# A decoder layer in split float32r: the second norm's broadcast as two float32r products for half the tokens, and two first transfers in the other order

## The chip, the cores and the metric

One core of one Trainium2 chip. The metric is the device time of one execution in microseconds, as the median of several runs. The profile is of one execution, with a span from the first to the last instruction that is a little shorter than its device time.

## The reference, cut to what matters

One layer (DEPTH = 1) of a decoder on x of 1024 tokens by 1024 features, all float32:

```python
u = rms_norm(h, attn_norm[i])
mix = swa_mixer(u, swa_w_qkv[j], swa_sinks[j], swa_w_o[j])
h = h + mix
h = h + squared_relu_mlp(rms_norm(h, mlp_norm[i]), mlp_w_up[i], mlp_w_down[i])
...
return rms_norm(h, final_norm)
```

`rms_norm` is `x * rsqrt(mean(x*x) + 1e-6) * g`. `swa_mixer` is attention in a window of 128 tokens, 16 query heads of 64 on 2 key and value heads, with a sink and a distance penalty for each head. `squared_relu_mlp` is `relu(h @ w_up)**2 @ w_down` with 4096 hidden features.

## The kernel before

Features lie on the partitions and tokens along the row, in tiles of 128 x 1024 (eight of them for x). Products are float32r in three parts: a value is split into a high part (a cast by ACT) and the rest (a subtraction by DVE), and `mm3` (line 131) adds high x high, high x low and low x high. The stages follow each other:

- **Keys and values** (lines 169 to 240): for each of the eight tiles k of x, ACT scales by the first norm's weights into `xh`, DVE makes the rest `xl`, and PE adds the products with tile k of the key and value weights into `psk` and `psv`. ACT also squares x, DVE adds the squares up in `ssq`, and small products with ones turn them into the sum for each token. The norm itself is applied later to keys, values and scores.
- **Attention** with the query products put between its steps, then **the output product** `o` (two blocks of 512 tokens, called hf = 0 and hf = 1, each for eight blocks m of features), which DVE adds onto `h`.
- **Second norm, and the up and down products** of the MLP in Strassen's form (seven products of half blocks, X, Y, Z in the profile being their banks), then the last norm.

The first transfers. Line 170 issues `gn` (all three norms' weights, 128 x 24) on ACT's queue and line 171 the first 256 columns of the key weights, `wk_r`, behind it. All other loads here are issued by SP: `xr`, the tiles of x (line 214; the first two tiles in halves of 512 tokens), and the other pieces of the key and value weights (`kvload`, line 188). `wsplit` (line 119) is the cast `wk_h` on ACT and the rest `wk_l` on DVE. The program writes the split of the first key weights ahead of the first `xh`; in this part the order on an engine is chosen by a scheduler, later (where `ordered` is set) it is the program's.

The second norm for hf = 0 runs under the output products of hf = 1. In the loop over m at line 917, with m = 0, `stat_part` puts small products with ones (`n2s`) between the twelve products of `oblock(0, 1)`; `stat_sum` (line 660) makes the reciprocal root `rn2` of each token with `rstd` (line 146: a root on ACT, then a Newton step on DVE, `n_st` in the profile) and a diagonal tile `dg` = identity x `rn2` with `diag` (line 157, DVE). With m = 1, behind the twelve products of `oblock(1, 1)`, `stat_bcast` (line 668) multiplies `dg` by ones (`bcast`, line 161: one float32 product of 128 x 512), so that every partition has the value of each token (`n2b`). DVE then makes `x` = h * gn * n2b, of which ACT and DVE make `xb_h` and `xb_l`. For hf = 1 the same happens later, under the first up products.

The first norm does its own broadcast (line 493) with a high part `rnh` and a rest `rnl` of the reciprocal root, two diagonals `dg1` in float32r, and two products with `ones_r`, a float32r copy of ones.

Of the kernel before, what the change touches and what calls it, by code (L numbers as in the profile page):

```python
# [6 lines left out]
F32 = mybir.dt.float32  # L7
F32R = mybir.dt.float32r
I32 = mybir.dt.int32
AF = mybir.ActivationFunctionType  # L10
ALU = mybir.AluOpType
# [3 lines left out]
P = 128  # L15
# [47 lines left out]
def trunk(tc, xT, gains, wqkv, wo, wup, wdn, bias_d, sinks_d, ident_d, mask_d, grow_d, outT, outB):  # L63
# [10 lines left out]
    nc = tc.nc  # L74
    v, s, g, pe = (Ordered(tc, e) for e in (nc.vector, nc.scalar, nc.gpsimd, nc.tensor))
# [14 lines left out]
    def wtile(dt, name):  # L90
        return big.tile([P, 1024], dt, tag="W", name=name, bufs=6)

    def rtile(name):
        return big.tile([P, 1024], F32, tag="R", name=name, bufs=3)
# [16 lines left out]
    def mm(out, lhsT, rhs, start, stop, **kw):  # L111
        pe.matmul(out, lhsT=lhsT, rhs=rhs, start=start, stop=stop, **kw)
        if tiny:
            tiny.pop(0)()
# [31 lines left out]
    def rstd(ps, n, name):  # L146
        st = const.tile([P, 4, NB], F32, tag="st", name=f"{name}_st", bufs=3)
        var, y0, b_, y = (st[:, i, 0:n] for i in range(4))
        s.activation(y, ps[:, 0:n], AF.Sqrt, bias=eps, scale=1.0 / DM)
        v.tensor_scalar(var, ps[:, 0:n], 1.0 / DM, EPS, op0=ALU.mult, op1=ALU.add)  # L150
        v.reciprocal(y0, y)
        v.tensor_tensor(b_, y0, y0, op=ALU.mult)
        v.scalar_tensor_tensor(b_, b_, -0.5, var, op0=ALU.mult, op1=ALU.mult)
        v.scalar_tensor_tensor(y, b_, 1.5, y0, op0=ALU.add, op1=ALU.mult)
        return y

    def diag(rn, b0, n, dg):
        v.tensor_tensor(dg[:, 0:n * P].rearrange("p (b c) -> p b c", b=n), ident.unsqueeze(1).to_broadcast([P, n, P]),
                        rn[:, b0:b0 + n].unsqueeze(2).to_broadcast([P, n, P]), op=ALU.mult)

    def bcast(n, ps, dg):
        mm(ps[:, 0:n * P], ones, dg[:, 0:n * P], True, True)
# [4 lines left out]
    pe.ordered = True  # L167

    wkv = [(rtile(f"{n}_r"), wtile(F32R, f"{n}_h"), wtile(F32R, f"{n}_l")) for n in ("wk", "wv")]
    nc.scalar.dma_start(gn, gains)  # L170
    nc.scalar.dma_start(wkv[0][0][:, 0:256], wqkv[8][:, 0:256])
    s.activation(rq, ones[:, 0:NB], AF.Square)
    warm = patt.tile([P, 512], F32, tag="pv", name="warm")
    for i in range(WARM):
# [2 lines left out]
    def small(tag, name):  # L177
        return patt.tile([P, 512], F32, tag=tag, name=name)
# [307 lines left out]
    rnh, ones_r = const.tile([P, NB], F32R, name="rnh"), const.tile([P, P], F32R, name="ones_r")  # L486
    rnl = const.tile([P, NB], F32, name="rnl")
# [11 lines left out]
    for hf in range(2):  # L499
        ps = small(("pv", "pt")[hf], f"n1_{hf}")  # L500
# [98 lines left out]
    mlp = tc.alloc_tile_pool(name="mlp", bufs=1)  # L599
# [5 lines left out]
    def bank(tag, name):  # L605
        if tag == "mm":
            return mmtile(name)
        return pml.tile([P, 512], F32, tag=tag, name=name, bufs=BANKS[tag])
# [10 lines left out]
    def sqtile(name):  # L619
        return mlp.tile([P, 512], F32, tag="sq", name=name, bufs=4)  # L620
# [26 lines left out]
    stat = {}  # L647
# [12 lines left out]
    def stat_sum(hf):  # L660
        while tiny:
            tiny.pop(0)()
        rn2 = rstd(stat["ps", hf], 4, f"n2_{hf}")
        dg = sqtile(f"dg2_{hf}")
        diag(rn2, 0, 4, dg)
        stat["dg", hf] = dg

    def stat_bcast(hf):
        ps = bank("Y", f"n2b{hf}")
        bcast(4, ps, stat.pop(("dg", hf)))  # L670
        return ps

    def square(m, hf):
# [230 lines left out]
    def oblock(m, hf):  # L904
        ps = bank(obanks[(hf * KT + m) % 5], f"o1_{m}_{hf}")
        for kk in range(4):
            mm3(ps, wsl(ws[m // 2], (m % 2) * 4 + kk), o_t[4 + kk], HALVES[hf], kk == 0, kk == 3)
        return ps
# [10 lines left out]
    for m in range(KT):  # L919
# [3 lines left out]
        ps = oblock(m, 1)  # L923
        if m == 0:
            stat_sum(0)
        if m == 1:
            rb = stat_bcast(0)
# [27 lines left out]
    WU["a11", 3], WU["a12", 3] = LO["wa3"]()  # L955
    bc = []
    up_mms(2, 0, {0: lambda: stat_sum(1)})
    up_mms(1, 1, {0: lambda: bc.append(stat_bcast(1))})
    rb = bc[0]
    snapshot(1, 1)  # L960
# [317 lines left out]
    for i, t0 in enumerate(tails):  # L1278
        ps = banks[2 + i]
# [62 lines left out]
```

## Time and profile before

| | |
|---|---|
| median of 3 runs | 924.63 us (924.92, 923.14, 924.63) |
| profiled execution, its own time | 923.56 us |
| its span | 921.9 us |
| PE busy | 905.8 us, 98% of the span |
| DVE, ACT, POOL busy | 690.6, 448.7, 281.4 us |
| granted TensorE clock, mean | 0.998 |
| DMA | 160.89 MB, mean 175 GB/s |

Times in the rows below are microseconds from the start of the span, unless ns is written. PE is TensorE's products, PEld its weight loads, DVE VectorE, ACT ScalarE, POOL GpSimd, SP SyncE; a name with q (ACTq, SPq) is the sequencer that issues transfers. A bracket at the end of a row is the idle time of that engine just before it and what released it. The starts of neighbouring products of PE overlap, so the time from one to the next is read from their starts or from the chain of waits, not from their durations. Almost every compute row has line 41, where a helper records it; rows are told apart by tiles.

### The profile page before, as it was taken

How to read it: one execution, taken by the hardware profiler on the slowest of the kernel's cores; microseconds unless marked ns; L12 is line 12 of the kernel's file. 1: busy time of each engine (PE TensorE's matmuls, PEld its weight loads, DVE VectorE, ACT ScalarE, POOL GpSimd, SP SyncE). 2: the span in 40 equal slices, each digit the busy share in tenths (PEclk: the TensorE clock that was granted, in tenths of full speed). 3: DMA queues.
4: the chain of work that ended last, by engine and by line, in shares of the span. 5: the costliest groups of instructions: out<-in, count | busy, mean ns of one | idle time of the engine just before them, and what ended most of it. 6: DMA issues, size and time to landing. Idle time of an engine off the chain costs nothing.

```text
span 921.9 us, 12421 instructions
## 1 busy us (share of the span) xinstructions
PE 905.8 (98%) x4410; PEld 759.2 (82%) x4410; DVE 690.6 (75%) x964; ACT 448.7 (49%) x861; POOL 281.4 (31%) x251
## 2 busy tenths in 40 slices
PE   8899999999999999999999999999999999999996
PEld 6788888888888787888888888788888888888995
DVE  7789988999858998866666575566878786467953
ACT  8578878877624364333333433343343333445421
POOL 1026656566245005654454434110000000031110
PEclk9999999999999999999999999999999999999999
DMA  8200100501354035645444444789888999547622
GB/s 315 69 29 29 53 24 13 205 30 46 112 179 168 1 109 188 221 145 168 164 147 141 143 170 169 272 308 409 300 325 293 333 347 317 179 150 267 258 92 92
DMA packets 57102, 160.89 MB, mean 175 GB/s; under 512 B 6480, under 2 KB 9296, under 8 KB 57040
## 3 DMA queue, kind: packets, MB, share of 16 engines
q1 hardware_dynamic: 56752, 159.95, 48.7%
q8 instruction: 35, 0.57, 0.3%
q14 instruction: 27, 0.22, 0.1%
q10 hardware_dynamic: 288, 0.14, 0.1%
HBM read 122.32 MB, written 37.75 MB: 174 GB/s over the span
## 4 chain that ended last, share of the span: by engine, by line
PE 89%; DVE 6%; ACT 2%; issue 1%; DMA 0%; ACTq 0%; DVEq 0%
PE d L41 33%; PE uX L41 16%; PE f L41 12%; PE uY L41 9%; PE o L41 5%; PE uZ L41 4%; PE pv L41 3%; PE S L41 3%; PE pt L41 1%; PE psv L41 1%; PE psk L41 1%; DVE h L41 1%; DVE ta L41 1%; DVE xt_l L41 1%; DVE oa L41 0%
## 5 line engine op out<-in xcount | busy, mean ns | idle before, releaser
L41 PE MATMUL d<-dx_h,dw_h 128*128 128x512 f32 (+1 forms) x448 | 168.0, 375 | 0.0
L41 PE MATMUL d<-dx_h,dw_l 128*128 128x512 f32 (+1 forms) x448 | 167.5, 374 | 0.0
L41 PE MATMUL d<-dx_l,dw_h 128*128 128x512 f32 (+1 forms) x448 | 167.5, 374 | 0.0
L41 PEld LDWEIGHTS d<-dx_l,dw_h 128*128 128x128 f32 x448 | 84.3, 188 | 15.3 <-issue 0.2
L41 PEld LDWEIGHTS d<-dx_h,dw_h 128*128 128x128 f32 x448 | 84.3, 188 | 15.3 <-issue 0.2
L41 PEld LDWEIGHTS d<-dx_h,dw_l 128*128 128x128 f32 x448 | 84.3, 188 | 14.8
L41 ACT CAST dw_h<-wf 128x1024 fp32r<-128x1024 f32 x40 | 41.9, 1051 | 95.7 <-PE d L41 79.5
L41 DVE TENSOR_TENSOR dx_l<-hr,dx_h 128x1024 fp32r<-128x1024 f32 x56 | 72.2, 1297 | 14.8 <-ACT dx_h L41 14.8
L41 ACT CAST dx_h<-hr 128x1024 fp32r<-128x1024 f32 x56 | 58.3, 1049 | 42.3 <-DMA hr<-hid 42.2
L41 POOL TENSOR_TENSOR ssq3a<-ssq3a,sq_a 128x512 f32<-128x512 f32 x7 | 11.7, 1667 | 209.6 <-ACT sq_a L41 209.2
L41 POOL TENSOR_TENSOR t<-t,sm 128x512 f32<-128x512 f32 x32 | 33.3, 1041 | 109.7 <-DVE sm L41 109.7
L41 DVE TENSOR_TENSOR wf<-wd,we 128x1024 f32<-128x1024 f32 x40 | 49.0, 1234 | 23.5 <-DMA we<-wdn 15.0
L41 DVE TENSOR_TENSOR dw_l<-wf,dw_h 128x1024 fp32r<-128x1024 f32 x40 | 48.7, 1220 | 22.3 <-ACT dw_h L41 22.1
L41 ACT ACTIVATE t<-t,sm 128x129 f32<-128x129 f32 x128 | 50.5, 397 | 11.1 <-DVE sm L41 10.6
L41 POOL TENSOR_TENSOR oc<-oc,oa 128x512 f32<-128x512 f32 x16 | 21.7, 1358 | 106.5 <-DVE oc L41 106.5
L41 PE MATMUL f<-xh,w_h 128*128 128x512 f32 x128 | 52.9, 413 | 0.0
L41 PE MATMUL f<-xl,w_h 128*128 128x512 f32 x128 | 50.4, 394 | 0.0
L41 PE MATMUL f<-xh,w_l 128*128 128x512 f32 x128 | 50.2, 392 | 0.0
L41 ACT COPY oa<-uX 128x512 f32<-128x512 f32 x32 | 18.8, 587 | 60.8 <-PE uX L41 60.8
L41 POOL TENSOR_TENSOR ob<-ob,oa 128x512 f32<-128x512 f32 x16 | 24.2, 1511 | 78.8 <-DVE ob L41 72.7
L41 PE MATMUL uX<-xu_h,wb 128*128 128x512 f32 x128 | 42.2, 391 | 0.7 <-ACT oa L41 0.7
L41 POOL TENSOR_SCALAR_AFFINE_SELECT cur<-hl 128x1024 fp32r<-128x1024 f32 x32 | 39.5, 1233 | 2.0 <-DVE hl L41 2.0
(386 smaller groups left out, 2445.9 us busy)
## 6 DMA issues: line engine op xcount, KB each, us to landing
wd<-wdn SPq DMA_DIRECT2D x56, 512.0 KB, 5.9
hr<-hid SPq DMA_DIRECT2D x56, 512.0 KB, 5.2
we<-wdn SPq DMA_DIRECT2D x40, 512.0 KB, 7.2
hid<-oa SPq DMA_DIRECT2D x32, 256.0 KB, 2.4
hid<-oc SPq DMA_DIRECT2D x32, 256.0 KB, 2.3
hid<-ob SPq DMA_DIRECT2D x32, 256.0 KB, 2.1
w_r<-wqkv SPq DMA_DIRECT2D x8, 512.0 KB, 3.7
h<-xT SPq DMA_DIRECT2D x8, 512.0 KB, 6.1
```

What stands on the lines that cost most here:

```text
L41: ins = method(*args, **kw)
```

## The change

Two edits. The two transfers of ACT's queue change places, so `wk_r` is issued first and `gn` second. For hf = 0, `rn2` is split into a high part (ACT) and a rest (DVE), in the tiles `rnh` and `rnl` that the first norm used; two diagonals are made, and the broadcast is two float32r products with `ones_r` in place of one float32 product with `ones`. For hf = 1 it stays as it was.

```diff
-    nc.scalar.dma_start(gn, gains)
     nc.scalar.dma_start(wkv[0][0][:, 0:256], wqkv[8][:, 0:256])
+    nc.scalar.dma_start(gn, gains)
...
         rn2 = rstd(stat["ps", hf], 4, f"n2_{hf}")
-        dg = sqtile(f"dg2_{hf}")
-        diag(rn2, 0, 4, dg)
+        if hf == 0:
+            hi, lo = rnh[:, 0:4], rnl[:, 0:4]
+            s.copy(hi, rn2)
+            v.tensor_tensor(lo, rn2, hi.bitcast(F32), op=ALU.subtract)
+            dg = []
+            for x in (hi.bitcast(F32), lo):
+                dg.append(mlp.tile([P, 512], F32R, tag="sq", name=f"dg2_{len(dg)}", bufs=4))
+                diag(x, 0, 4, dg[-1])
+        else:
+            dg = sqtile(f"dg2_{hf}")
+            diag(rn2, 0, 4, dg)
         stat["dg", hf] = dg
 
     def stat_bcast(hf):
         ps = bank("Y", f"n2b{hf}")
-        bcast(4, ps, stat.pop(("dg", hf)))
+        dg = stat.pop(("dg", hf))
+        if hf == 0:
+            for i in range(2):
+                mm(ps, ones_r, dg[i], i == 0, i == 1)
+        else:
+            bcast(4, ps, dg)
         return ps
```

What it moves on the engines, at three places. The first is the start of ACT's order, with its two transfers (`xh_111` is the first tile of `xh`, in two halves). Before:

```order
L170 DMA gn<-gains 128x24
L171 DMA wk_r<-wqkv 128x256
L41 ACT_TABLE_LOAD
L41 ACTIVATE rq<-ones 128x8
L41 CAST ones_r<-ones 128x128
L41 ACTIVATE xh_111<-xr_102,gn 128x512
L41 CAST wk_h<-wk_r 128x256
L41 ACTIVATE xh_111<-xr_102,gn 128x512
L41 CAST wv_h<-wv_r 128x256
```

After the change:

```order
L170 DMA wk_r<-wqkv 128x256
L171 DMA gn<-gains 128x24
L41 ACT_TABLE_LOAD
L41 ACTIVATE rq<-ones 128x8
L41 CAST wk_h<-wk_r 128x256
L41 ACTIVATE xh_111<-xr_102,gn 128x512 x2
L41 CAST wv_h<-wv_r 128x256
```

The cast of the key weights moves ahead of both halves of `xh`, and the cast of `ones_r` moves away, ahead of the `xh` of the fourth tile. DVE follows: its `wk_l` moves ahead of the first `xl`.

The second place is DVE at the second norm of hf = 0, from the end of the reciprocal root (`n_0_st`) to the first residual add (`h_2055`):

```order
 L41 TENSOR_TENSOR n_0_st<-n_0_st 128x4
 L41 SCALAR_TENSOR_TENSOR n_0_st<-n_0_st 128x4 x2
-L41 TENSOR_TENSOR dg_0_3180<-ident,n_0_st 128x512
+L41 TENSOR_TENSOR rnl<-n_0_st,rnh 128x4
+L41 TENSOR_TENSOR dg_0_3182<-ident,rnh 128x512
+L41 TENSOR_TENSOR dg_1_3184<-ident,rnl 128x512
 L41 TENSOR_TENSOR h_2055<-o_0_1_3148,h_2055 128x512
```

One diagonal becomes a subtraction and two diagonals, in front of the same adds; on ACT the cast `rnh` comes in behind the root, ahead of the squares of `h_2055`.

The third place is PE behind the twelve products of `oblock(1, 1)`. Before:

```order
L41 MATMUL o_1_1_3195<-ol_2753,wo_0_h 128x512
L41 MATMUL o_1_1_3195<-oh_2752,wo_0_l 128x512
L41 MATMUL n2b_3208<-dg_0_3180,ones 128x512
L41 MATMUL o_2_1_3224<-oh_1887,wo_1_h 128x512
L41 MATMUL o_2_1_3224<-ol_1888,wo_1_h 128x512
```

After the change:

```order
L41 MATMUL o_1_1_3199<-ol_2753,wo_0_h 128x512
L41 MATMUL o_1_1_3199<-oh_2752,wo_0_l 128x512
L41 MATMUL n2b_3212<-dg_0_3182,ones_r 128x512
L41 MATMUL n2b_3212<-dg_1_3184,ones_r 128x512
L41 MATMUL o_2_1_3229<-oh_1887,wo_1_h 128x512
L41 MATMUL o_2_1_3229<-ol_1888,wo_1_h 128x512
```

One product becomes two; what stands before and behind them is the same. Everything else on every engine, SP and POOL among them, stands in the same order as before.

## Rows read from the trace of the kernel before

**Rows 1.** The page: busy time of each engine with its share of the span and its instructions, and the chain that ended last, by engine.

```profile
PE 905.8 (98%) x4410; PEld 759.2 (82%) x4410; DVE 690.6 (75%) x964; ACT 448.7 (49%) x861; POOL 281.4 (31%) x251
...
PE 89%; DVE 6%; ACT 2%; issue 1%; DMA 0%; ACTq 0%; DVEq 0%
```

**Rows 2.** What PE waited for in the whole span: us in total, times, the longest. Behind them the granted clock of a long stretch (the number before the DMA share).

```profile
PE vt L41 <- DVE vv L41: 2.4, 2, 1.7
PE psk L41 <- DVE xl L41: 1.2, 2, 0.7
...
PE psk L41 <- ACT wk_h L41: 1.0, 1, 1.0
...
16.00:44.00 28.00, 25.45 (x119) 20.33 (x118) 23.10 (x37) 18.92 (x29) 0.00 (x0) 1.00 0.38 138
```

**Rows 3.** The chain that ended last, its first pieces: start, duration, what.

```profile
1.24 4.14 DMA wk_r<-wqkv
```

**Rows 4.** ACT in order of time in the first 14 us: start, duration, instruction, idle time before it.

```profile
3.13 0.28 ACT L41 CAST ones_r<-ones 128x128 fp32r<-128x128 f32 x1
3.85 0.72 ACT L41 ACTIVATE xh<-xr,gn 128x512 fp32r<-128x512 f32 x1 [0.44 <-DMA gn<-gains]
5.40 0.40 ACT L41 CAST wk_h<-wk_r 128x256 fp32r<-128x256 f32 x1 [0.83 <-DMA wk_r<-wqkv]
5.71 0.72 ACT L41 ACTIVATE xh<-xr,gn 128x512 fp32r<-128x512 f32 x1
6.34 0.39 ACT L41 CAST wv_h<-wv_r 128x256 fp32r<-128x256 f32 x1
...
13.41 1.14 ACT L41 ACTIVATE xh<-xr,gn 128x1024 fp32r<-128x1024 f32 x1
```

**Rows 5.** Transfers by their issue, each asked for by a window of its own: the first two issued at 0.81 (SP) and 0.80 (ACT), then, by SP, 1.24 and 1.71. Columns: what, queue, KB, us from issue to landing.

```profile
xr<-xT SPq DMA_DIRECT2D x1, 256.0 KB, 2.8
gn<-gains ACTq DMA_DIRECT2D x1, 12.0 KB, 3.0
...
xr<-xT SPq DMA_DIRECT2D x1, 256.0 KB, 4.0
wv_r<-wqkv SPq DMA_DIRECT2D x1, 128.0 KB, 3.8
```

**Rows 6.** DMA packets between 2.5 and 2.9: all of them, then by queue (q1 is SP's, q10 ACT's) with MB and share of the 16 DMA engines.

```profile
DMA packets 134, 0.14 MB, mean 348 GB/s; under 512 B 69, under 2 KB 69, under 8 KB 134
...
q1 hardware_dynamic: 67, 0.13, 90.4%
q10 hardware_dynamic: 67, 0.01, 12.3%
```

**Rows 7.** DVE, then PE, in order of time from 8 to 17 us; the last row is PE's.

```profile
8.33 1.42 DVE L41 SCALAR_TENSOR_TENSOR xl<-xr,gn,xh 128x512 fp32r<-128x512 f32 x2 [0.78 <-ACT xh L41]
...
10.51 1.23 DVE L41 TENSOR_TENSOR ssq<-ssq,sq 128x1024 f32<-128x1024 f32 x1
...
15.19 1.28 DVE L41 SCALAR_TENSOR_TENSOR xl<-xr,gn,xh 128x1024 fp32r<-128x1024 f32 x1
...
16.53 0.50 PE L41 MATMUL psk<-xl,wk_h 128*128 128x512 f32 x1 [0.50 <-DVE xl L41]
```

**Rows 8.** What SP's issues waited for in the first 14 us: us in total, times, the longest (L189 is the load of key and value weights).

```profile
SPq L189 <- DMA wk_r<-wqkv: 0.7, 1, 0.7
...
SPq L189 <- DMA gn<-gains: 0.3, 1, 0.3
```

**Rows 9.** DVE, then ACT, in order of time around the second norm of hf = 0, and DVE's wait at the end of the output products.

```profile
272.66 0.36 DVE L41 SCALAR_TENSOR_TENSOR n_st<-n_st 128x4 f32<-128x4 f32 x2
273.05 0.69 DVE L41 TENSOR_TENSOR dg<-ident,n_st 128x512 f32<-128x512 f32 x1
273.66 0.68 DVE L41 TENSOR_TENSOR h<-o,h 128x512 f32<-128x512 f32 x1
274.77 0.69 DVE L41 TENSOR_TENSOR h<-o,h 128x512 f32<-128x512 f32 x1 [0.42 <-PE o L41]
275.63 2.72 DVE L41 SCALAR_TENSOR_TENSOR x<-h,gn,n2b 128x512 f32<-128x512 f32 x4 [0.17 <-PE n2b L41]
...
291.96 0.69 DVE L41 TENSOR_TENSOR h<-o,h 128x512 f32<-128x512 f32 x1 [0.77 <-PE o L41]
...
274.44 0.63 ACT L41 ACTIVATE sq<-h 128x512 f32<-128x512 f32 x1 [2.29 <-DVE h L41]
```

**Rows 10.** The chain that ended last around the second norm: start, duration, what, and how many instructions.

```profile
274.73 0.86 PE n2b L41 x2
275.59 16.33 PE o L41 x72
...
302.12 1.41 DVE h L41 x2
```

**Rows 11.** The first norm's split: ACT's cast (all instructions that write or read the tile: count, min/median/max ns, first and last start), then DVE in order of time.

```profile
L41 ACT CAST rnh<-n_st x1: 198/198/198, 35.0 to 35.0; 128x8 fp32r<-128x8 f32 x1
...
35.20 0.17 DVE L41 TENSOR_TENSOR rnl<-n_st,rnh 128x8 f32<-128x8 f32 x1
35.28 0.68 DVE L41 TENSOR_TENSOR dg<-ident,rnh 128x512 fp32r<-128x512 f32 x1
35.88 0.68 DVE L41 TENSOR_TENSOR dg<-ident,rnl 128x512 fp32r<-128x512 f32 x1
```

More of the change, by code (lines that the diff above doesn't have):

```diff
@@ L169, in trunk @@
     wkv = [(rtile(f"{n}_r"), wtile(F32R, f"{n}_h"), wtile(F32R, f"{n}_l")) for n in ("wk", "wv")]
+    nc.scalar.dma_start(wkv[0][0][:, 0:256], wqkv[8][:, 0:256])
     nc.scalar.dma_start(gn, gains)
-    nc.scalar.dma_start(wkv[0][0][:, 0:256], wqkv[8][:, 0:256])
     s.activation(rq, ones[:, 0:NB], AF.Square)
```

## The prediction

> **What bounds the kernel now.** I read the page first, then who PE waits for, then the chain of waits at the start, then the two places that the change touches. The page has PE busy for 905.8 us of a span of 921.9 us, and the chain that ended last runs through PE for 89% [rows 1]. So a step counts only where PE itself does less, or where PE stands still. The list of what PE waits for is short: about 2.2 us on the first key and value products, 2.4 us on the transposes of the values, and little else [rows 2]. Both parts of the change lie near an entry of that kind: one in the first 6 us, one on PE's own work at 274 us.
>
> The start. The chain begins with one transfer: the first 256 columns of the key weights (wk_r), issued by ACT at 1.24, landing 4.14 us later, at 5.38 [rows 3]. ACT then casts them (wk_h, 5.40). Ahead of that ACT has done the first half of xh (3.85, released by the gains gn), and has stood still for 0.83 us [rows 4]. From 5.40 on ACT shows no idle time in its rows; DVE's xl of 8.33 waits for ACT's xh, its first sum of squares (10.51) follows ACT's sq, and from there DVE runs without a gap to the xl that PE waits for at 16.53 [rows 4, 7]. After that PE is ahead until it waits for the values. So the moment at which ACT starts the second half of xh (5.71 now) carries over to PE at 16.53, microsecond for microsecond, as long as no load comes late.
>
> The second norm. At 274.73 PE spends 0.86 us on n2b, the broadcast of the first half; 72 float32r products of the same 512 columns behind it take 16.33 us, 0.227 us each [rows 10]. PE has no wait there.
>
> **The broadcast (hf = 0).** On PE, 0.86 goes and 2 x 0.227 = 0.45 comes: 0.40 us less on the path. That holds if both diagonals are ready. Now the reciprocal root is finished by DVE at 272.66 + 0.36 = 273.02 and the diagonal runs from 273.05 to 273.74 [rows 9]. The first norm does the new steps already: ACT's cast rnh takes 0.198 us, rnl starts 0.2 us behind it, the first diagonal 0.08 behind rnl, the second 0.60 behind the first and lasts 0.68 [rows 11]. Put behind 273.02: cast 273.07, rnl 273.27, high diagonal 273.35 to 274.03, low diagonal 273.95 to 274.63. PE gets to its first product at 274.57 as before, and to the second 0.23 later, at 274.80. So there is 0.17 us of room and no wait. ACT's cast falls into 2.29 us in which ACT waits anyway [rows 9], and no table load stands between the root and the squares behind it in the order now.
>
> Behind the diagonals on DVE stand the residual adds h and the products x. The adds move from 273.66 and 274.77 to 274.55 and 275.15, x from 275.63 to 275.76: 0.13 us later, while PE is 0.40 earlier. The cover is DVE's wait of 0.77 us for PE at 291.96 [rows 9]; of it 0.77 - 0.40 - 0.13 = 0.24 us are left, so DVE has caught up before PE needs the x of this half in the first up products. If that cover were short, PE would wait there for the rest, up to 0.53 us. The second half's broadcast stays as it is, and behind it (302.12 on) the chain runs through DVE [rows 10]; it hangs on n2b of the second half, which comes 0.40 us earlier because PE does. **Term: -0.40 us.** Bounds: 0 if the low diagonal is late by that much, -0.45 if both products pipeline into their neighbours fully.
>
> **The two transfers.** The change takes gn out of the front of ACT's queue and puts wk_r there; ACT's order becomes wk_h, then both halves of xh. What ACT does is the same; what it waits for first is not wk_r but gn. Call the landing of gn G. Then the first half of xh starts at G + 0.02 (both casts of now start 0.02 to 0.05 behind their landing), the second half 0.63 later, which is the pitch of 5.71 to 6.34 in the rows [rows 4]. Now it starts at 5.71. So the difference is **G - 5.06**: a gain if gn lands ahead of 5.06, a loss behind it.
>
> No row shows gn as the second transfer of its queue, so G has to be bounded. From below: gn took 3.0 us from issue to landing [rows 5]; issued at 1.24 that is 4.24. The second half of xh needs its own x (xr), issued 1.24, landing 4.0 later, so it can't start before 5.2 then: a gain of 0.5. From above: the next transfer of SP's queue, wv_r, lands at 1.71 + 3.8 = 5.5: a loss of 0.44. Which end is nearer? The rows show pairs: the first xr (0.81 + 2.8 = 3.6) with gn (3.8), the second xr (5.2) with wk_r (5.4). The one on ACT's queue came in 0.2 behind its partner both times. The packets of the two queues explain it: between 2.5 and 2.9 they moved 67 and 67, one for one, small or not, so 128 packets of gn need the 128 packets of xr beside them [rows 6]. After the change wk_r is beside the first xr (384 KB in place of 268; 116 KB at 348 GB/s is 0.33 us, so wk_r lands near 4.15 and its cast is over at 4.55), and gn is beside the second xr. The bytes in front of the end of both pairs are the same as now, so the second pair lands when it lands now, 5.2 to 5.4. I take G = 5.3. **Term: +0.24 us.**
>
> The Trainium skill (DMA: Bandwidth & Descriptors, section Queues, rings and completion order) says that a DMA engine drains a whole packet, typically 9 to 17 descriptors, from one queue's ring before it turns to the next. The trace's one-for-one counts don't show that [rows 6]. By the rule gn would stand wholly behind the second xr, as wk_r does now, at 5.38: a term of +0.32 and a sum of -0.08.
>
> What else moves there. The cast ones_r leaves ACT's idle time at 3.13 and comes in ahead of the xh of 13.41: 0.28 us, covered by the 0.64 us between that xh's end (14.55) and DVE's use of it (15.19) [rows 4, 7]. SP's next loads wait for the landings of gn (0.3 us) and wk_r (0.7 us) [rows 8]; these two now swap places, so the first of them goes out some 0.3 us later and the second as now. From 5.40 on ACT waits for no load in its rows, so I give that no price; what would cover a later load is the time that it lies landed before ACT takes it, and without that cover the cost is at most those 0.3 us. PE's first gap on the key weights grows from 1.0 us to about 1.2; a gap of 1.7 us passes in a stretch whose granted clock is 1.00 (2.4 GHz) [rows 2], so I give it no price either.
>
> **Sum:** -0.40 + 0.24 = -0.16 us. The profiled execution took 923.56 us (span 921.9), so 923.40 by its own account; it lies 1.07 below the median of 924.63. The four executions known have a mean of 924.06, the better guess of where the next ones fall: 924.06 - 0.16 = **923.9 us**. A measurement of this kernel can tell about 0.2%, 1.85 us; the sum is a tenth of that.
>
> **Rivals.**
> (a) gn is quick also as the second transfer, because it is only 12 KB: G from 4.24 to 4.8. For: its 3.0 us. Against: the one-for-one packets. The start gains 0.5, the sum is -0.9: 923.2. Chance 0.22.
> (b) Slower: gn lands still later, beside wv_r. The place is ACT's wait in front of the first xh; it decides from G = 5.46, where the loss of 0.40 eats the broadcast's gain, and each 0.1 us more costs 0.1 us, through ACT and DVE to PE at 16.53. At 5.5 to 5.7 the sum is +0.04 to +0.24: 924.1 to 924.3. For: ACT's transfers trail SP's by 0.2 us in both pairs. Against: the bytes ahead of it are no more than those ahead of wk_r now (5.38). Chance 0.16.
> (c) The change doesn't do what it says on PE: the low diagonal comes later than 275.2, PE waits out what it saves, and the sum is +0.24: 924.3. For: 0.17 us of room only, behind a hop to ACT and back. Against: the same steps' durations at 35 us. Chance 0.07.
> The forecast has 0.50, and 0.05 is left for what I don't see.
>
> **Range and chances.** The low end is the lowest run, 923.14, with rival (a) and the far bound of the broadcast, -0.95: 922.2. The high end is the highest run, 924.92, with the far bound of each term, +0.44 and 0: 925.4. No case moves the time by 1.85 us; what is left for faster (0.08) and slower (0.05) is the spread of the runs around the median (1.8 us between three of them), more on the faster side since the median shown lies above the mean and three quarters of the cases are gains.
>
> **What would show it.** On the changed kernel: n2b of the first half as two products that take about 0.45 us on the chain, at 274 us plus or minus the start's term, with no wait of PE for dg; ACT's wk_h near 4.2, the first xh at G, with its wait put down to gn; PE's last wait for xl at 16.53 + (G - 5.06), 16.8 by the forecast; the n2b of the second half earlier by the sum. I am wrong on the start if the first xh starts ahead of 5.0, and on the broadcast if PE waits for dg or if PE shows a new wait for xb_l at the first up products.

## The result and the profile after

| | before | after |
|---|---|---|
| median | 924.16 us (20 executions, 923.14 to 926.56) | 925.62 us (20 executions, 923.95 to 927.59) |
| ratio | | 1.0013, 95% interval 1.0007 to 1.0019 |
| profiled execution, its own time | 923.56 us | 926.04 us |
| its span | 921.9 us | 924.3 us |

The change makes the kernel slower, by 0.6 to 1.8 us. That is less than the 0.2% I called measurable, but with twenty executions of each the interval leaves out no change. I had forecast 923.9, 0.16 faster than the mean of the four executions I knew, in a range to 925.4; the median is past its end.

The two profiles are 2.4 us apart. The page of after, PE's share and the chain by engine, answers to [rows 1]: PE is busy 3.2 us longer over the same 4410 instructions, so something made its products longer.

```profile
PE 909.0 (98%) x4410; PEld 762.3 (82%) x4410; DVE 690.9 (75%) x966; ACT 448.7 (49%) x862; POOL 281.9 (30%) x251
...
PE 88%; DVE 8%; ACT 2%; DMA 1%; issue 1%; POOL 0%; ACTq 0%; DVEq 0%; POOLq 0%; SPq 0%
```

What PE waits for in after, against [rows 2]: us in total, times, the longest.

```profile
PE vt L41 <- DVE vv L41: 2.4, 2, 1.7
...
PE psk L41 <- ACT xh L41: 1.0, 1, 1.0
...
PE n2s L41 <- POOL sq L41: 0.5, 1, 0.5
```

Two things are new. The first key product is released by `xh`, so by the gains, and no longer by `wk_h`; and there is a wait that before does not show, of PE for POOL's sums of squares of the second half (n2s). The wait for xl is gone. I take the three places in order of time.

**The start.** The chain of after begins with another transfer than in [rows 3]; then ACT (against [rows 4]) and the landings (against [rows 5]: issued at 0.81 by SP, 0.80 by ACT, then 1.24 by SP and 1.25 by ACT).

```profile
1.25 4.20 DMA gn<-gains
```

```profile
4.62 0.40 ACT L41 CAST wk_h<-wk_r 128x256 fp32r<-128x256 f32 x1 [1.39 <-DMA wk_r<-wqkv]
5.54 1.33 ACT L41 ACTIVATE xh<-xr,gn 128x512 fp32r<-128x512 f32 x2 [0.51 <-DMA gn<-gains]
```

```profile
xr<-xT SPq DMA_DIRECT2D x1, 256.0 KB, 3.6
wk_r<-wqkv ACTq DMA_DIRECT2D x1, 128.0 KB, 3.8
...
xr<-xT SPq DMA_DIRECT2D x1, 256.0 KB, 4.0
...
gn<-gains ACTq DMA_DIRECT2D x1, 12.0 KB, 4.2
```

The 12 KB of gains took 4.2 us in second place; they had taken 3.0 in first [rows 5]. By the chain they landed at 5.45, 0.2 behind the second `xr`; the first `xh` started at 5.54, so G counts as 5.52 in the prediction's own sum. The second half of `xh` starts at 5.54 + 0.63 = 6.17 instead of 5.71, 0.45 late. DVE carries it as [rows 7] said: its first sum at 10.95 (10.51), its xl at 15.62 (15.19).

**The second norm.** DVE in after, in order of time, against [rows 9]; the first row is the two-operand product ahead of those shown there.

```profile
274.61 0.36 DVE L41 TENSOR_TENSOR n_st<-n_st 128x4 f32<-128x4 f32 x1
275.01 0.36 DVE L41 SCALAR_TENSOR_TENSOR n_st<-n_st 128x4 f32<-128x4 f32 x2
275.63 0.16 DVE L41 TENSOR_TENSOR rnl<-n_st,rnh 128x4 f32<-128x4 f32 x1 [0.26 <-ACT rnh L41]
275.71 0.69 DVE L41 TENSOR_TENSOR dg<-ident,rnh 128x512 fp32r<-128x512 f32 x1
276.31 0.69 DVE L41 TENSOR_TENSOR dg<-ident,rnl 128x512 fp32r<-128x512 f32 x1
276.92 1.28 DVE L41 TENSOR_TENSOR h<-o,h 128x512 f32<-128x512 f32 x2
```

From the root's end to the end of the low diagonal it takes 1.63 us; the prediction had 1.61. But the first product of four columns takes 0.36. In before that same row is short. Before, DVE; then POOL of before and PE's first n2s of the second half:

```profile
272.46 0.16 DVE L41 TENSOR_TENSOR n_st<-n_st 128x4 f32<-128x4 f32 x1
```

```profile
271.22 1.28 POOL L41 TENSOR_TENSOR sb<-wu1c,sa 128x512 f32<-128x512 f32 x1
...
291.47 1.30 POOL L41 TENSOR_TENSOR sq<-sq,sq 128x512 f32<-128x512 f32 x1 [0.32 <-ACT sq L41]
```

```profile
292.44 0.39 PE L41 MATMUL uX<-xb_h,wa_h 128*128 128x512 f32 x1
292.82 0.38 PE L41 MATMUL n2s<-ones,sq 128*128 128x1 f32 x2
```

And the same of after, POOL and PE:

```profile
273.68 1.28 POOL L41 TENSOR_TENSOR sb<-wu1c,sa 128x512 f32<-128x512 f32 x1
...
293.94 1.29 POOL L41 TENSOR_TENSOR sq<-sq,sq 128x512 f32<-128x512 f32 x1 [0.31 <-ACT sq L41]
```

```profile
295.29 0.38 PE L41 MATMUL n2s<-ones,sq 128*128 128x1 f32 x2 [0.48 <-POOL sq L41]
```

Read two sums here. POOL's up-weight sum ends at 273.68 + 1.28 = 274.96 and DVE's small product, begun at 274.61, at 274.97. And POOL's last add of squares ended at 292.77 before, and PE's first n2s started at 292.82; now it ends at 295.23 and n2s starts at 295.29, and PE shows 0.48 of idle time. From the first n2b product to the first one of the second half it is 26.39 us before (274.57 to 300.96) and 26.71 after (276.71 to 303.42): the broadcast costs 0.32 where I had a gain of 0.40.

PE's first n2s starts 0.05 behind the end of POOL's last add in both kernels. That was no room before but a wait already: the product ahead of it starts at 292.44, so n2s comes 0.38 behind it where the other products follow 0.23 apart. The 0.15 between does not show as idle time, because it lies under the modelled end of that product. So PE stands behind POOL at this place in both kernels, and POOL behind ACT and DVE. The rows of that chain, DVE and ACT of before, then of after:

```profile
289.92 1.27 DVE L41 TENSOR_TENSOR h<-o,h 128x512 f32<-128x512 f32 x2
...
290.69 0.63 ACT L41 ACTIVATE sq<-h 128x512 f32<-128x512 f32 x1 [1.10 <-DVE h L41]
```

```profile
292.40 1.28 DVE L41 TENSOR_TENSOR h<-o,h 128x512 f32<-128x512 f32 x2
...
293.17 0.63 ACT L41 ACTIVATE sq<-h 128x512 f32<-128x512 f32 x1 [1.10 <-DVE h L41]
```

These rows and POOL's add are 2.47 or 2.48 later in after, and DVE's first product x is 2.48 later too (278.11 for 275.63), with no idle time of DVE from there to this add. PE is 2.14 later at the first n2b. The difference, 0.34, is what DVE has lost at the diagonals, and it comes out at PE as the 0.32.

**The clock.** Windows of before, then of after, over the value transposes: PE busy, PEld, DVE, ACT, POOL, granted clock, DMA share, GB/s.

```profile
41.00:44.70 3.70, 1.35 (x6) 0.88 (x7) 3.42 (x8) 2.22 (x5) 0.00 (x0) 1.00 0.00 0
44.70:48.20 3.50, 3.50 (x21) 2.78 (x20) 1.41 (x4) 1.82 (x5) 0.00 (x0) 1.00 0.00 0
```

```profile
41.00:44.70 3.70, 1.80 (x8) 0.84 (x6) 3.54 (x7) 2.98 (x7) 0.00 (x0) 1.00 0.00 0
44.70:48.20 3.50, 3.01 (x8) 2.26 (x9) 1.36 (x5) 0.73 (x2) 0.00 (x0) 0.51 0.00 0
```

In after's profiled execution the granted clock falls to its lower level, 1.2 GHz, at 44.7 us for 3.41 us, behind a stretch in which PE waits for the transposes. The last transpose stands at 49.83 instead of 47.66: 2.17 later, of which 0.81 was there at the last key product (29.26 against 28.45). That is 1.36 of the 2.4 us. The experiments show that the same fall comes in executions of the kernel before; whether the change makes it more frequent they leave open.

Of the 0.81, 0.45 is the later `xh`. The other 0.36 I put on a late rise of the clock at the start: in after the products of 512 columns still follow each other 0.43 us apart at 9.4 to 10.3 and are 0.23 apart from 10.65 on; the trace's record of the full clock, 2.4 GHz, begins at 10.59. In before they are 0.23 apart at 7.6 already, and that record begins at 4.15. (A window gives 1.00 ahead of the record too, so the distance of the products is the sign.)

### The profile page after: what moved, and what is told of

The parts are those of the page before. It is cut to its first block, busy times and chain, and to the rows that moved or that the text cites. A ratio compares the mean times of both kernels' runs of the same rounds, so it can differ in the third digit from the quotient of the medians.

```text
span 924.3 us, 12422 instructions
## 1 busy us (share of the span) xinstructions
PE 909.0 (98%) x4410; PEld 762.3 (82%) x4410; DVE 690.9 (75%) x966; ACT 448.7 (49%) x862; POOL 281.9 (30%) x251
## 4 chain that ended last, share of the span: by engine, by line
PE 88%; DVE 8%; ACT 2%; DMA 1%; issue 1%; POOL 0%; ACTq 0%; DVEq 0%; POOLq 0%; SPq 0%
PE d L41 33%; PE uX L41 16%; PE f L41 13%; PE uY L41 9%; PE uZ L41 4%; PE pv L41 3%; PE o L41 3%; PE S L41 3%; PE psk L41 1%; PE pt L41 1%; PE psv L41 1%; DVE x L41 1%; DVE h L41 1%; DVE ta L41 1%; DVE xb_l L41 1%
```

## The experiments

My theory: 0.45 from the gains in second place, 0.32 from the broadcast by way of POOL's sums, the rest from a late rise and a fall of the clock that come in some executions. The rivals: the clock falls because of the change; the broadcast's two products are themselves slow.

| run | median, us | lowest to highest | before beside it |
|---|---|---|---|
| e1 swap alone | 925.36 | 923.72 to 925.81 | 924.54 |
| e2 broadcast alone | 923.88 | 923.38 to 928.13 | 924.54 |
| e3 broadcast, later sums | 924.64 | 923.09 to 925.33 | 924.54 |
| e4 later sums alone | 924.75 | 923.17 to 925.39 | 924.54 |
| e5 broadcast, POOL freed | 923.99 | 923.23 to 925.18 | 923.59 |
| e6 query steps in the gap | 929.66 | 927.34 to 930.00 | 923.59 |
| e7 key weights on SP | 924.11 | 923.61 to 925.52 | 923.59 |
| e8 low diagonal on ACT | 923.46 | 923.07 to 924.92 | 923.59 |
| e9 spare products in the gap | 923.42 | 923.16 to 923.65 | 923.70 |
| e10 change + e9 | 924.47 | 923.92 to 927.69 | 923.70 |
| e11 e10 + 2 warm products | 924.30 | 923.91 to 924.57 | 923.70 |
| e12 e5 + e8 + e9 | 922.99 | 922.89 to 923.71 | 923.70 |
| e13 swap + e9 + 2 warm | 924.04 | 923.88 to 924.71 | 923.46 |
| e14 broadcast + e9 | 923.50 | 923.31 to 924.86 | 923.46 |
| e15 e9 + 2 warm | 923.32 | 923.15 to 923.70 | 923.46 |
| e16 swap + e9 | 924.26 | 923.74 to 924.43 | 923.46 |
| e17 e10 again | 924.17 | 924.00 to 925.26 | 924.05 |

Each has 11 executions (e2 and e10 12, e6 5), the kernel before 15 to 35 beside them. Runs e1 to e4 had one chip, e5 to e16 a second and e17 a third; the lowest time of the kernel before beside them is 923.09, 923.11 and 923.14.

**e1, the swap alone.**

```diff
-    nc.scalar.dma_start(gn, gains)
     nc.scalar.dma_start(wkv[0][0][:, 0:256], wqkv[8][:, 0:256])
+    nc.scalar.dma_start(gn, gains)
```

> The two transfers in the changed order, the broadcast as before. Theory (start and sums): gn lands near 5.5 again, ACT starts the second half of the first xh near 6.15 in place of 5.71, so everything behind is later by 0.44 us, and by up to 0.4 more if PE's granted clock rises late; no wait of PE for POOL's sum of squares; fastest runs 0.4 to 0.8 us above the fastest of before, ratio 1.0005 to 1.0009. Rival (the start is harmless, the whole loss is behind 42 us): fastest runs within 0.15 us of before's.

The second half of `xh` starts at 6.00, the last key product at 28.90 (28.45 before), and the stretch from n2b to n2b is 26.40, with no more wait for POOL than before. So the start's loss is the swap's, and the n2s wait is not. The median is not told apart from before (1.0006, 0.9997 to 1.0014).

**e2, the broadcast alone** (the second hunk of the change).

> The broadcast for hf = 0 as two float32r products, the transfers in the order of before. Theory (sums): the two products are 0.2 to 0.4 us shorter than the one, but DVE's adds of h come 0.9 us later, the squares and POOL's running sum of them follow, and PE waits 0.4 to 0.6 us for that sum at the first n2s of hf = 1: from n2b of hf = 0 to n2b of hf = 1 it takes 26.8 us in place of 26.5, the run is slower by 0.1 to 0.3 us. Rival (the broadcast does what was forecast, the loss is the start's alone): no wait there, 26.1 us, faster by 0.4 us.

```profile
292.95 0.38 PE L41 MATMUL n2s<-ones,sq 128*128 128x1 f32 x2 [0.48 <-POOL sq L41]
```

The wait for POOL's sq is there, the two products take 0.68 on PE's time line, and n2b to n2b is 26.72. The loss at the second norm belongs to the broadcast.

**e3 and e4, the products n2s three products later**, behind the second of the four blocks of the first up product instead of the first, with the broadcast and without:

```diff
-    up_mms(1, 0, {0: lambda: [stat_part(1, i) for i in range(3)]})
+    up_mms(1, 0, {1: lambda: [stat_part(1, i) for i in range(3)]})
```

> The broadcast as two float32r products, transfers as before, and the products n2s of hf = 1 put three products of PE later (behind the second block of the first up product in place of the first), which gives POOL's sum 0.69 us more. Theory (sums): PE's wait for POOL is gone, 26.1 to 26.4 us from n2b of hf = 0 to n2b of hf = 1, faster than the broadcast alone by 0.5 us and than before by 0.2 to 0.4. Rival (the wait has another cause, or DVE's lateness appears at the next place, the products x or xb_l): still 26.7 or more, no faster than the broadcast alone.

> Control: the kernel before with the products n2s of hf = 1 three products later and nothing else. Theory (sums): POOL's sum was there 0.05 us ahead of PE before, so nothing is gained: 26.5 us from n2b to n2b, the same time within 0.1 us. Rival: a shorter way by itself (26.3 or less), so that a gain of the broadcast with the same move is not the broadcast's.

In e3 the wait for POOL is gone and nothing is gained: n2b to n2b is 26.78. The wait has turned into another. What PE waits for around the second norm, then DVE and POOL at the second root:

```profile
PE n2b L41 <- DVE dg L41: 0.4, 1, 0.4
```

```profile
298.69 0.35 DVE L41 TENSOR_TENSOR n_st<-n_st 128x4 f32<-128x4 f32 x1
299.07 1.42 DVE L41 SCALAR_TENSOR_TENSOR n_st<-n_st 128x4 f32<-128x4 f32 x2
```

```profile
297.75 1.27 POOL L41 TENSOR_TENSOR wu2b<-wu2b 128x512 f32<-128x512 f32 x1
298.98 1.29 POOL L41 TENSOR_TENSOR wu2c<-wu2c,s 128x512 f32<-128x512 f32 x1
```

DVE's products of four columns end when POOL's running sum ends: 299.04 for 299.02, and the first of the two behind it at 300.29 by its own row, for POOL's 300.27. The first root was held too, for 0.66, and the two n2b products there cost 0.94. e4 leaves the stretch at 26.40 as expected. Its profile also has the clock rising late (10.48) and falling at 44.62, with the transfers in their old order.

**e5, one of POOL's sums on DVE**, with the broadcast:

```diff
-        g.tensor_tensor(sa[:, 1], rw[:, 0], rw[:, 1], op=ALU.add)
+        if p != 1:
+            g.tensor_tensor(sa[:, 1], rw[:, 0], rw[:, 1], op=ALU.add)
...
+            rw1, sa1, _ = SUM[1]
+            v.tensor_tensor(sa1[:, 1], rw1[:, 0], rw1[:, 1], op=ALU.add)
```

> The broadcast alone, as two float32r products, and one of GpSimd's four sums on the second pair of up weights (sa[:,1], 128x512) given to VectorE, behind its last sum h of the first half, where VectorE was idle from 267.1 to 272.0 us. GpSimd's last sum before the second norm then ends near 271.3 instead of 272.6. Theory (VectorE's small two-operand instructions don't end before GpSimd's running instruction does): the first TENSOR_TENSOR n_st takes 0.16 instead of 0.36, the low diagonal is done 0.2 earlier after the first n_st, and the two n2b products take 0.45 on TensorE's time line instead of 0.68; from the first n2b product to the one of the second half 26.72 -> 26.5, with TensorE's wait for GpSimd's sums of squares still there (0.4 to 0.6), since everything behind moves with it. Rival (the 0.36 is due to the two float32r diagonals or to the added cast, not to GpSimd): n_st still 0.36, two products 0.68, 26.7. Median not told apart from e2's 923.9 (0.2 us less at most).

POOL, then DVE, of e5:

```profile
270.32 1.27 POOL L41 TENSOR_TENSOR sb<-wu1c,sa 128x512 f32<-128x512 f32 x1
```

```profile
271.99 0.16 DVE L41 TENSOR_TENSOR n_st<-n_st 128x4 f32<-128x4 f32 x1
```

As expected: POOL is done at 271.59, the product takes 0.16, the two n2b products start 0.24 apart, and n2b to n2b is 26.50, with the 0.48 at n2s still there. So 0.2 of the cost is POOL's hold. How much DVE is held depends on when POOL's sum ends and differs between executions: the product takes 0.36 in after, e2 and e10, 0.66 in e3, 0.21 in e17 and 0.16 in e11 and e14.

**e8, the low diagonal on ACT**, with the broadcast:

```diff
-                diag(x, 0, 4, dg[-1])
+                if x is lo:
+                    for b in range(4):
+                        s.activation(dg[-1][:, b * P:(b + 1) * P], ident, AF.Copy, scale=lo[:, b:b + 1])
+                else:
+                    diag(x, 0, 4, dg[-1])
```

> The broadcast alone, its low diagonal built by ScalarE as four scaled copies of the identity (128x128 each, about 0.33 each by the vv copies) instead of one 0.69 product of VectorE. Theory (TensorE's new wait of 0.5 at the sums of squares is VectorE's lateness, handed on through ScalarE's squares to GpSimd's adds): VectorE is 0.6 earlier at the sums h, the wait for GpSimd's sq falls from 0.48 to 0.0 to 0.2, and from the first n2b product to the second half's it is 26.72 -> 26.2 to 26.4, at or below the kernel before (26.39). The two products may still take 0.7, since ScalarE ends the low diagonal at about 274.8. Rival (GpSimd's adds are late for their own reason, or ScalarE's longer work makes the squares late): the wait stays at 0.4 to 0.6 and the stretch at 26.7. Median 923.5 to 924.3 beside about 923.9 to 924.5 of the kernel before: not told apart.

PE, then POOL, of e8:

```profile
292.97 0.38 PE L41 MATMUL n2s<-ones,sq 128*128 128x1 f32 x2
```

```profile
291.62 1.30 POOL L41 TENSOR_TENSOR sq<-sq,sq 128x512 f32<-128x512 f32 x1 [0.31 <-ACT sq L41]
```

PE's row shows no idle time: 0.6 us less on DVE took away 0.48 on PE. POOL's hold is missing in e8 as well (DVE's product takes 0.16), but so it is in e5, where the 0.48 stayed. n2b to n2b is 26.13, a little under what I expected and 0.26 under before. So PE's new wait was DVE's second diagonal, handed on through ACT's squares to POOL.

The starts say it more simply. DVE's first x begins 1.06 behind the first n2b product in before, 1.40 in e2, 1.19 in e5 and 0.81 in e8; against before that is +0.34, +0.13 and -0.25, and the stretch is +0.33, +0.11 and -0.26. The two move together, within 0.04, in every profile but e3's, where the sums stand elsewhere.

**e7, the key weights on SP's queue**, kernel before otherwise:

```diff
-    nc.scalar.dma_start(wkv[0][0][:, 0:256], wqkv[8][:, 0:256])
...
+                kvload(0, slice(0, 256))
```

> The kernel before with the first key weights' transfer taken off ScalarE's queue and issued by SyncE between the two halves of the first xr; the gains are alone on ScalarE's queue. Theory (packets are drained one for one from the two queues, so the second of two transfers on ScalarE's queue is held behind the large ones beside it): wk_r lands near 4.4 instead of 5.4, right behind the first half of xr, the second half of xr near 5.2, ScalarE's second xh starts at 5.2 to 5.4 instead of 5.71, and the last psk product moves 0.3 to 0.5 down from 28.45. Rival (SyncE's issues are what sets the landings): xr's second half is one issue of 0.43 later and the second xh starts at 5.9 to 6.2. ScalarE and VectorE also do one pair of wv splits one place later. Time: 923.9 to 924.2 against 924.5 by the first, 924.8 by the second; the two groups of times of 1.6 us apart, by the granted clock at 44 us, stay.

A miss. `wk_r` came by 4.41, as expected, but the second half of `xr` not at 5.2:

```profile
4.41 0.39 ACT L41 CAST wk_h<-wk_r 128x256 fp32r<-128x256 f32 x1
6.21 0.72 ACT L41 ACTIVATE xh<-xr,gn 128x512 fp32r<-128x512 f32 x1 [1.42 <-DMA xr<-xT]
```

It was issued at 1.71 and took 4.5 us. The lower times are some 0.5 us above before's.

**e6, three query steps moved into the gap**, kernel before otherwise:

```diff
-        fill(1)
+        fill((1, 1, 2, 3, 1, 1, 1, 1)[n])
```

> The kernel before with three more steps of the first query projections (three products each, 0.70 us) put where TensorE idles before the attention loop: one ahead of the third, two ahead of the fourth of the value transposes (waits of 0.70 and 1.70 there). The rest of the order moves up by three steps. Theory (the 1.6 us between the two groups of times of every kernel is the granted clock falling to 1.2 GHz for 3.4 us from 44.7 us, in executions where TensorE has idled at 41 to 44): no fall there in the profile, and all times in one group; the median falls by 0.8 us, and by up to 2.1 us more if the attention loop is held by TensorE. Rival (the clock's groups come from elsewhere, and the attention loop is held by other engines): the two groups stay 1.6 apart, and the median moves under 0.5 us, or up where the query steps run out earlier at the loop's end.

A miss in the time: the median is 6.1 us above before's (by the ratio 4.7), and I had given no size for a loss. In the attention loop PE waits 3.0 us for DVE's `c`, against 0.3 in before, and near the loop's end, where the query steps run out earlier, 2.0 for `h`. The clock fell there too. Windows of e6:

```profile
233.00:236.00 3.00, 0.98 (x5) 0.58 (x4) 2.99 (x6) 0.88 (x4) 1.48 (x2) 1.00 0.47 153
236.40:239.90 3.50, 3.50 (x14) 2.91 (x13) 1.57 (x4) 1.46 (x6) 1.55 (x3) 0.51 0.00 0
```

At 44.7 it did not fall. The fall has moved with the idle stretch.

**e9, eight spare products in the gap**, kernel before otherwise; no work is moved:

```diff
+    spare = patt.tile([P, 4, 256], F32, tag="S", name="spare", bufs=2).rearrange("p a b -> p (a b)")
...
+        for i in range({2: 2, 3: 6}.get(n, 0)):
+            mm(spare[:, 0:512], ones_r, xg[0][0][:, 0:512], True, True)
```

> The kernel before with eight extra products (ones_r by xh, 512 columns, 0.227 us each, their result is read by nothing) where TensorE waits for the value transposes: two ahead of the third (wait of 0.70), six ahead of the fourth (1.70). No work is moved. Theory (the two groups of times, 1.6 us apart, are executions without and with a fall of the granted clock at 44.7 us, behind TensorE's idle stretch at 41 to 44): the fall is gone, nearly all executions fall in the lower group, 923.1 to 923.8, and the median is 0.0 to 1.2 below that of the kernel before beside it, by the share of upper times that it happens to have. Rival (the groups have another cause): about half of the executions at 924.5 to 925.4 as before.

```profile
41.00:44.70 3.70, 3.17 (x15) 2.31 (x15) 3.02 (x7) 2.19 (x5) 0.00 (x0) 1.00 0.00 0
44.70:48.20 3.50, 3.50 (x23) 2.87 (x21) 1.41 (x4) 1.84 (x6) 0.00 (x0) 1.00 0.02 5
```

PE is busy 3.17 of the 3.70 us, the clock stays, and all eleven times lie within 0.5 us. Over all runs the kernel before has 70 of its 163 executions above 924.3 us; e9, e12, e14 and e15, which have the spare products and the old order of transfers, have one of 44. That one (e14, 924.86) has a mean granted clock of 0.999, so it is no fall. For 143 of the 163 the mean granted clock is on record: 0.9983 below 924.3 and 0.9962 above, and a fall of 3.41 us to half in a span of 922 makes 0.0018. So the upper group is in the main the executions with the fall, and the kernel before has it too.

**e10 and e17, the whole change with the spare products; e11, two warm products more** (`WARM = 11` for 9).

> The changed kernel, whole, with the same eight extra products. Theory (the change by itself costs 0.45 at the start and 0.32 at the second norm, and up to 0.4 where the clock rises late; the rest of the 1.5 between the medians is the share of executions in which the clock falls at 44.7): one group of times at 923.9 to 924.3, that is 0.6 to 0.8 above the lower group of e9_gap_spare. Rival (the change itself makes the clock fall more often): times at 925.5 and more remain in half of the runs.

> The kernel of e10 (the changed kernel with the eight extra products) once more. If both edits together have slow executions of their own, a third to a half of these are above 924.6 again, and their profile, if one is caught, has a stretch of lower clock or a late start of over 1 us. If e10's five were a matter of that hour, all are at 923.9 to 924.6, 0.7 to 1.0 over e9, as e11 and e16 are.

> e10_after_gap_spare with eleven products ones by ones ahead of the first key product instead of nine, so that TensorE works up to the first key product at 6.3 us (nine end at 5.33 at the lower clock, 0.47 each). Theory (the late rise of the granted clock, at 10.6 instead of 4.2 us, comes with TensorE's longer first gap and costs the first products 0.36): the clock rises before 6.5, the last psk product ends 0.3 to 0.4 earlier than 29.26, and the lower times are 923.5 to 924.0. Rival (the rise is a matter of when the execution starts, as it is late in e4 with the gap of before): the rise stays anywhere from 4 to 11 and the time where e10 has it.

The change costs 0.75 to 1.05 us over e9 (924.17 to 924.47 against 923.42). e11 is in one group, 0.88 over e9. Its clock rises at 5.21, as the theory had it, but the last key product stands at 29.24 and not 0.3 earlier: PE waits for xl instead (1.4 us, three times). That doesn't refute the price of the late rise, since in this execution ACT waits for the third tile of x:

```profile
11.24 1.15 ACT L41 ACTIVATE xh<-xr,gn 128x1024 fp32r<-128x1024 f32 x1 [0.50 <-DMA xr<-xT]
```

The other profiles price it. Where the clock rises no later than 7.1 and no load is late, the last key product comes 22.73 to 22.77 behind the second half of the first `xh` (ten profiles). In the four with a rise near 10 or later and no late load it comes 22.90 (e1), 22.98 (e10), 23.05 (e4) and 23.09 (after) behind, so the late rise goes with 0.15 to 0.35. With the nine warm products it is late in four of the five profiles with the swap and in one of ten with the old order; whether the swap brings it, so few don't show.

e10 and e17 together have 7 of 23 executions above 924.6 and e11 none of 11. What these seven do is open. Two, at 927.6 and 927.7, have a mean granted clock of 0.994, so their clock fell somewhere; the others have 0.996 to 0.999. The one profiled, of e17 (924.79), has a late start, its last key product at 29.50, where ACT had waited 0.59 for the third tile of x.

**e12, a version from what had paid:** the old order of transfers, e5, e8 and e9 together.

> A version of what the runs so far pay for: the order of the first transfers of the kernel before; the broadcast as two float32r products with its low diagonal on ScalarE (e8); one of GpSimd's sums given to VectorE (e5); the eight extra products of e9. From the first n2b product to the second half's 25.9 to 26.2 (26.39 before, 26.13 in e8), so 0.3 to 0.5 below e9_gap_spare: 922.6 to 923.4, all in one group, and 0.3 to 1.8 below the kernel before's median. If the low diagonal on ScalarE becomes what TensorE waits for, the two products take 0.6 to 0.7 and the gain over e9 is 0.1 to 0.3.

922.99 us, 0.9991 of before (0.9982 to 0.9999): the one version whose whole interval lies under 1. n2b to n2b is 26.15, 0.24 under e9's 26.39, as expected; the times differ by 0.43, and the 0.2 between is no more than the scatter of either.

**e13 to e16, the parts with the gap filled.** e13 is e1 with e9 and `WARM = 11`, e14 is e2 with e9, e15 is e9 with `WARM = 11`, e16 is e1 with e9.

> The swap of the two transfers alone, with the eight extra products of e9 and eleven products ones by ones at the start as in e11. Theory (the swap costs 0.45 to 0.7 at the start: the last key product stands at 28.43 in the mean of nine profiles with the transfers of before, at 29.10 in the mean of four with the swap): one group, its median 0.45 to 0.7 above e15_gap_warm, 923.9 to 924.2. Rival (the swap's cost is given back before the attention loop, and the 0.88 between e11 and e9 is the broadcast's): within 0.2 of e15.

> The broadcast alone with the eight extra products of e9. Theory (it costs 0.32 between the first n2b product and the second half's, by GpSimd's late sums): one group, its median 0.2 to 0.4 above e9_gap_spare's 923.42, at 923.6 to 923.8. Rival (the wait at the sums is given back by the end, the broadcast is free): 923.3 to 923.5. By my prediction's step it would be 0.40 less than e9: 923.0.

> The kernel before with the eight extra products and eleven products ones by ones at the start: the control for e13. Its first key product can start near 5.4 to 5.9 and the eleven end at 4.9 to 5.8, so they should cost nothing: 923.2 to 923.6, one group, as e9. If they end behind the first key weights (lower clock, 0.47 each from 1.12 us: 6.3), up to 0.4 more.

> The swap alone with the eight extra products of e9 and the nine products at the start as before. Theory (the scatter of e10 above 924.6 comes with the swap, by TensorE's longer idle stretch ahead of the first key product and the late rise of the clock): lower times at 923.9 to 924.2 and a quarter to a half of the executions 0.5 to 3.5 above. Rival (it comes with the broadcast): one narrow group like e13's.

The swap costs 0.72 (e13 against e15) and 0.84 (e16 against e9); e16 scatters by 0.7 us and no more, so the swap alone does not bring back e10's tail. The broadcast costs 0.08 without the swap (e14 against e9) and 0.26 with it (e11 against e13), never -0.40; the two ranges overlap both times, and the 0.08 is not told apart from nothing. In both profiles, e14's and e11's, n2b to n2b is 26.49, 0.10 above before: POOL's last sum ended at 272.28 in e14 and held DVE's product (272.17, 0.16) hardly at all.

The swap's price also shows why one profile misled me. ACT at the start of e15, with the old order, and of e16, with the new:

```profile
4.88 0.41 ACT L41 CAST wk_h<-wk_r 128x256 fp32r<-128x256 f32 x1 [0.39 <-DMA wk_r<-wqkv]
5.19 0.72 ACT L41 ACTIVATE xh<-xr,gn 128x512 fp32r<-128x512 f32 x1
```

```profile
4.41 0.40 ACT L41 CAST wk_h<-wk_r 128x256 fp32r<-128x256 f32 x1 [1.18 <-DMA wk_r<-wqkv]
5.35 1.34 ACT L41 ACTIVATE xh<-xr,gn 128x512 fp32r<-128x512 f32 x2 [0.54 <-DMA gn<-gains]
```

In the eleven profiles with the old order (before, e2 to e6, e8, e9, e12, e14, e15) the second half of `xh` starts between 5.19 and 6.00, 5.47 in the mean; in the seven with the swap (after, e1, e10, e11, e13, e16, e17) between 5.94 and 6.17, 6.04 in the mean. The difference is 0.57, and at the last key product 0.68 (28.36 and 29.04), with the late rises and the late loads of x in it. The one profile that I read had 5.71.

## Why the prediction was wrong, step by step

**Transfers, +0.24: right in mechanism and sign, mis-sized.** G was 5.52 in after and about 5.4 in the mean of the seven; 5.3 was near. The reference failed: "G - 5.06" took `wk_r` at 5.38 from the one profiled execution, and in the others with that order its cast starts at 4.88 to 5.69. The cast `wk_h`, forecast near 4.2, came at 4.62, without effect, since ACT then waited 0.51 for the gains. Measured, the term is +0.57 at ACT, +0.72 to +0.84 in the time. The mechanism held: in before and in after the second transfer of ACT's queue lands 0.2 behind the second `xr`, be it 12 KB or 128. By the Trainium skill's rule (DMA: Bandwidth & Descriptors, section Queues, rings and completion order), that whole packets go in turn, G would have been 5.38; the landings don't tell the two apart.

**Broadcast, -0.40: wrong in sign.** The step that failed is "The cover is DVE's wait of 0.77 us for PE at 291.96 ... so DVE has caught up before PE needs the x of this half in the first up products". I followed x, and PE indeed shows no wait for `xb_l`. But the same lateness of DVE's adds h goes through ACT's squares to POOL's sums, which PE needs first. The add that feeds POOL's last sum, at 289.92, stands ahead of the wait that I took for cover, and PE already stood behind POOL there. The rows were in the trace of before (POOL's add to 292.77, PE at 292.82, the product ahead at 292.44); I had not read POOL at all. So nothing that PE saved at the products could count, and DVE's delay counted in full. The 0.13 that I had put on x was right (+0.13 in e5, with +0.11 on the stretch); POOL's hold made it 0.34 in after, and the stretch +0.32. In time it is +0.08 to +0.26.

**"0.17 us of room and no wait": right behind the root's end, which came 0.2 late.** The steps took 1.63 for 1.61. POOL's running sum held the product in front of them, and the two products cost 0.68 instead of 0.45 (e2), or 0.47 when POOL is done in time (e5: from the first of them to the last output product of the half 16.59 us, 0.37 less than before's 16.96). Rival (c) had this place but not this cause, and rival (b) a start that costs more than I forecast.

**"No price" for PE's longer first gap and for the clock.** That gap did not grow (0.98 for 1.03), but the clock rose late in after, and such a rise goes with 0.15 to 0.35 at the last key product. A late load of x, which I gave no price either, held ACT in two of the seven profiles with the swap (0.50 and 0.59) and in two of the twelve without (0.18 and 0.84), so it is not the swap's. The fall at 44.7 costs about 1.4 us where it comes, in 43% of the executions of before. In after 13 of 20 lie above 924.7; whether the change has a part in that share is not shown, since e1 has 6 of 11 above 924.7 and e10 and e17 have a tail without the gap. My range took in the spread of three executions, and not that the median can fall in either group.

In sum: +0.72 to +0.84 for the swap and +0.08 to +0.26 for the broadcast make 0.8 to 1.1, against 0.75 to 1.05 measured with the gap filled; what the 1.46 between the medians has above that I put on the share of executions with the fall and on e10's tail, which no run tells apart.

## What to carry to other kernels

Before an edit on one engine is priced by who uses its main result, follow every output of the delayed engine to the first place where the bound engine needs it, and read from the starts whether it already waits there: here PE already stood behind a chain over three engines, with no idle time in its rows, so that chain decided and not PE's own work. Take the reference of a start-up race from more than one execution if there are any; a difference to one profile inherits that profile's luck. And where times fall in two groups, look for an idle stretch of PE behind which the granted clock falls: eight products that nobody reads put 11 of 11 executions in the lower group.

## What the hardware did that I had not expected

- DVE's small instructions with two operands in SBUF do not end before POOL's running sum does: 0.36 for 0.16 (after), 0.90 in before at the second half's root (298.81 to 299.71, POOL's sum to 299.69), and 1.42 for a pair that takes 0.36 alone (e3). TENSOR_SCALAR and RECIPROCAL of the same size, 0.16 and 0.17, were not held. The Trainium skill (SBUF — State Buffer, section SBUF: two separate sides) says that DVE with two SBUF inputs and POOL take turns on one pair of ports, each for a whole instruction; the trace agrees.
- The same gap of PE (1.70 us, behind one of 0.70) is followed by a fall of the granted clock in some executions and not in others: PE was busy 1.35 of 3.70 us in before, without a fall, and 1.80 in after, with one.
- A transfer of 12 KB in second place of its queue takes as long as one of 128 KB there: 4.0 to 4.2 us (seven profiles), against 2.9 to 3.0 in first place; one of 128 KB took 3.6 to 4.4 in second place.
